# A hybrid decoder layer on one core: GpSimd's large operations to VectorE and ScalarE, Y evicted straight into its block tile, A's gates beside the SSD, x's first tile loaded first

## The chip, the cores and the metric

The kernel runs on one core of a Trainium2 chip. TensorE (PE) multiplies matrices, VectorE (DVE), ScalarE (ACT) and GpSimd (POOL) do the rest, and SyncE (SP) issues most of the DMAs. Each engine takes its instructions strictly in the order in which they stand on its queue, and waits on semaphores for the other engines. The metric is the device time of one execution in microseconds, the median of the runs taken.

## The reference, cut to what matters

One layer for a prompt of 1024 tokens and 8 samples of 8 tokens (1088 columns in all, T). One projection feeds four head groups, and a second one mixes them:

```python
z = jnp.einsum('bld,de->ble', x, p['w_in'])          # 1024 -> all columns of A, B, C, D
(a_x, a_gate, b_xbc, b_dt, b_gate, c_qkv, c_beta, c_decay, c_gate, d_u, d_gate) = split_cols(z, IN_SPLITS)
ya = rglru_mixer(a_x)  * silu(a_gate)                # A: conv of width 4, gated linear scan
yb = rms_norm(ssd_mixer(b_xbc, b_dt) * silu(b_gate)) # B: Mamba-2 SSD, chunked scan, 4 heads x 64
yc = gdn_mixer(c_qkv, c_beta, c_decay) * silu(c_gate)# C: gated DeltaNet, chunked
yd = s5_mixer(d_u) * silu(d_gate)                    # D: S5, 16 groups x 64 complex states
out = concat(ya, yb, yc, yd) @ w_out
x = layer_norm(ALPHA * x + out)
# inside gdn_mixer, for each chunk and head: a triangular inverse
tmat = triangular_solve(eye + m, eye, lower=True, unit_diagonal=True)
value, kcum = tmat @ (beta * v), tmat @ (beta * exp(decay) * k)
# inside s5_mixer: h_t = a * h_{t-1} + B u_t (complex, diagonal), y = Re(C h) + D u
```

The new states of the convs, the scans and S5 are returned as well.

## The kernel before

Each of x's eight k-tiles (128x1088) is split into a high part `xh` (ACT) and a low part `xl` (DVE); each weight strip likewise into `wh` and `wl`. A strip of 128 output columns is three blocks of tokens (320, 384, 384), each of 8 x 3 matmuls (xh.wh, xl.wh, xh.wl: L226 to L228 for most strips, L374 to L376 for S5's input, L398 to L400 for the token-major strip of small columns). Work comes in this order:

- **Start.** SP's queue loads the first halves of two S5 weight strips (`wr`), then x's first three k-tiles; POOL's queue loads `s5p`, `hv`, `pcol`. PE begins with S5's input strips (`pu`, L374).
- **S5's tables and the token strip.** DVE builds S5's constants, then `table(0)`, the powers of the state's factor (doubling, 42 small complex products, L463 to L465 in `cmul`). `outs(hf)` (L618 to L620) are six products of 128x512 on POOL. `half_run(hf)` multiplies by the table (`cm`, `gd`), scans (L650), multiplies back into `H`, and PE forms `y` from `H` and `outs` (L672, L676). `gemm_tok` runs beside half 0: nine token blocks of 24 matmuls (L398), each emptied by ACT (L403 to L406), gated by DVE (L407) and sent to DRAM (`bgd`) from a rotating buffer `bg`. `table(1)` and `outs(1)` are both on POOL and go on beside the gemms of C's strips.
- **C's strips** go through `gemm_strip`, `conv_of` and norms. `copy_out` empties PSUM: three copies of four on ACT (L242), the fourth on DVE (L244). `keep_tail` copies each strip's last columns on POOL (L270, L271).
- **The chunks of C** (from 208 us): for each of 8 prompt chunks of 128 tokens and one of 64, `prep` and `invert`, then `state`. `invert` runs six levels (three for the short chunk, 51 in all) of a block inversion for 4 heads. In one level PE forms T (L855), DVE masks it into `T` (L857) and copies its two diagonal blocks into `tb` (L846); PE accumulates X (L862), ACT evicts it (L864); PE accumulates Y (L867), ACT evicts it (L868); DVE copies Y's two diagonal blocks into `yb` (L846, `spread`), which the next level's L862 needs as its stationary side. `al`, the low part of A, comes from POOL (L839), as does `kd` (L801).
- **Beside the chunks** a second stream, `side`, gives PE its long matmuls: A's RG-LRU with the SSD's strips (`ahead`) merged in, then A's two gate strips, the SSD's four convs, and the SSD's chunks merged with the four gate strips of D and C (`gates_cd`). `merge` deals out yields by shares written beside each stream. `project` multiplies by w_out (L1426 to L1428) and does the LayerNorm: DVE adds and takes statistics, POOL raises to the power (L1437) and applies gain and bias (L1443, L1444), except for the last tile, where DVE does it (L1448, L1450).

A scheduling layer fixes each engine's order while the program is built; what an engine executes is that list, in order.

## Time and profile before

| | us |
|---|---|
| median of 3 runs | 653.14 |
| the runs | 653.14, 647.74, 653.92 |
| the profiled execution | 648.38 |
| its span, first to last instruction | 646.5 |
| PE busy | 589.7 (91%) |
| DVE busy | 469.6 (73%) |
| ACT busy | 271.6 (42%) |
| POOL busy | 180.9 (28%) |

The profile is one execution. Of each engine it tells the busy time, what ended each idle stretch (the releaser), and the clock granted to PE (1.00 is 2.4 GHz, half of that 1.2 GHz). Idle time counts only on an engine that the end of the program waits for, so PE's waits are read first, with their place in time. Busy time of PE is modelled from starts and sizes.

### The profile page before, as it was taken

Reading aid. Unit: us, or ns where it says so; the run is one execution under the profiler, and the core shown is the slowest. Engines: PE = TensorE matmul, PEld = TensorE weight load, DVE = VectorE, ACT = ScalarE, POOL = GpSimd, SP = SyncE. Lnnn points to the kernel's source line nnn. Section 1 sums busy time; section 2 is a strip of 40 time slices with the busy share of each in tenths; the row PEclk is TensorE's granted clock in tenths of the full one; section 3 lists DMA queues with packets and bytes.
Section 4 is the critical chain, followed back from the end, with each engine's and each line's share of the span. In section 5 each row is a group of like instructions: output and inputs, shape, how many; then the busy total and the mean of one; then the engine's idle time right before and its main releaser. Section 6 shows DMA issues by size and latency. Waiting matters only on the chain.

```text
span 646.5 us, 11718 instructions
## 1 busy us (share of the span) xinstructions
PE 589.7 (91%) x4284; PEld 504.0 (78%) x4284; DVE 469.6 (73%) x1378; ACT 271.6 (42%) x677; POOL 180.9 (28%) x305
## 2 busy tenths in 40 slices
...
GB/s 288 165 191 63 41 34 86 1 96 59 128 57 55 18 36 33 33 18 19 33 69 68 33 89 66 1 17 43 9 75 78 171 43 49 33 55 113 66 117 78
DMA packets 23929, 44.11 MB, mean 68 GB/s; under 512 B 3073, under 2 KB 10193, under 8 KB 23873
## 3 DMA queue, kind: packets, MB, share of 16 engines
q1 hardware_dynamic: 23696, 42.71, 20.1%
...
## 4 chain that ended last, share of the span: by engine, by line
PE 66%; DVE 19%; POOL 5%; issue 5%; ACT 2%; DMA 1%; SPq 0%; DVEq 0%; ACTq 0%; POOLq 0%
PE pg L226 8%; PE pg L227 8%; PE pg L228 8%; PE pg L1428 5%; PE pg L1427 5%; PE pg L1426 5%; DVE tb L846 2%; DVE yb L846 2%; DVE acc L266 2%; PE ssq L755 1%; PE pg L398 1%; DMA x<-in_x_t_dram 1%; PE pg L399 1%; PE pg L400 1%; PE kq L817 1%
## 5 line engine op out<-in xcount | busy, mean ns | idle before, releaser
L226 PE MATMUL pg<-xh,wh 128*128 128x384 f32 (+1 forms) x432 | 150.2, 348 | 9.0 <-DVE z L244 9.0
L227 PE MATMUL pg<-xl,wh 128*128 128x384 f32 (+1 forms) x432 | 149.0, 345 | 0.0
L228 PE MATMUL pg<-xh,wl 128*128 128x384 f32 (+1 forms) x432 | 147.0, 340 | 0.0
L226 PEld LDWEIGHTS pg<-xh,wh 128*128 128x128 f32 x432 | 82.8, 192 | 12.5 <-DVE z L244 9.3
L227 PEld LDWEIGHTS pg<-xl,wh 128*128 128x128 f32 x432 | 82.6, 191 | 2.1 <-issue 0.5
L228 PEld LDWEIGHTS pg<-xh,wl 128*128 128x128 f32 x432 | 82.4, 191 | 1.3 <-issue 0.3
L1426 PE MATMUL pg<-woh,wh 128*128 128x512 f32 (+1 forms) x144 | 58.2, 404 | 1.9 <-ACT wh L1415 1.9
L1427 PE MATMUL pg<-wol,wh 128*128 128x512 f32 (+1 forms) x144 | 58.5, 406 | 0.2
L1428 PE MATMUL pg<-woh,wl 128*128 128x512 f32 (+1 forms) x144 | 57.9, 402 | 0.4 <-DVE wl L1416 0.4
L266 DVE SCALAR_TENSOR_TENSOR acc<-z,pcol,acc 128x1112 f32<-128x1112 f32 x36 | 49.6, 1381 | 5.1 <-ACT acc L264 4.8
L864 ACT ACTIVATE XY<-XY 128x256 f16<-128x256 f32 (+1 forms) x51 | 19.4, 381 | 53.8 <-PE XY L862 48.2
L156 ACT ACTIVATE wh<-wr 128x512 fp32r<-128x512 f32 (+1 forms) x40 | 25.2, 633 | 35.0 <-PE pg L227 28.3
L1429 DVE SCALAR_TENSOR_TENSOR y<-y,pg 128x512 f32<-128x512 f32 (+1 forms) x18 | 12.3, 686 | 32.2 <-PE pg L1428 28.4
L1426 PEld LDWEIGHTS pg<-woh,wh 128*128 128x128 f32 (+1 forms) x144 | 26.6, 184 | 8.9 <-ACT wh L1415 2.2
L1428 PEld LDWEIGHTS pg<-woh,wl 128*128 128x128 f32 (+1 forms) x144 | 26.6, 185 | 7.3 <-DVE wl L1416 0.9
L1427 PEld LDWEIGHTS pg<-wol,wh 128*128 128x128 f32 (+1 forms) x144 | 26.5, 184 | 7.2 <-DVE wol L1393 1.0
L157 DVE TENSOR_TENSOR wl<-wr,wh 128x512 fp32r<-128x512 f32 (+1 forms) x40 | 28.2, 704 | 2.8 <-ACT wh L156 2.4
L857 DVE TENSOR_TENSOR T<-T,lev 128x256 f16<-128x256 f32 (+1 forms) x51 | 21.4, 419 | 10.7 <-PE T L855 10.1
L868 ACT ACTIVATE XY<-XY 128x256 f16<-128x256 f32 (+1 forms) x51 | 19.4, 381 | 22.5 <-PE XY L867 22.5
L242 ACT ACTIVATE z<-pg 128x384 f32<-128x384 f32 (+2 forms) x37 | 14.0, 389 | 34.5 <-PE pg L228 33.2
L846 DVE COPY tb<-T 64x256 f16<-64x256 f16 x99 | 26.2, 264 | 1.6
L846 DVE COPY yb<-XY 64x256 f16<-64x256 f16 x99 | 23.8, 240 | 4.4 <-ACT XY L868 3.0
...
## 6 DMA issues: line engine op xcount, KB each, us to landing
...
```

The costliest lines, as they stand in the source:

```text
L156: act(hv_, wv, AF.Copy)
L157: lo_eng[0].tensor_tensor(lv, wv, hv_.bitcast(F32), OP.subtract)
L226: mm(o, whi[k], xh[:, k, a:b], start=(k == 0), stop=False)
L227: mm(o, whi[k], xl[:, k, a:b], start=False, stop=False)
L228: mm(o, wlo[k], xh[:, k, a:b], start=False, stop=(k == 7))
L266: stt(acc[:, :CL], s[:, j:j + CL], col(wkey, j * nt + i), acc[:, :CL], OP.mult, OP.add)
L846: V.tensor_copy(dst[s, :, s], src[s])
L857: tt(t_[:n], pt[:n], lev[:n, l].unsqueeze(1).to_broadcast([n, 4, 64]), OP.mult)
L864: act(XY[:n, :256], px[:n, :256], AF.Copy)
L1426: mm(ps[:n], mh[k_], woh[:, k_, e], start=(k_ == 0), stop=False)
L1427: mm(ps[:n], mh[k_], wol[:, k_, e], start=False, stop=False)
L1428: mm(ps[:n], ml[k_], woh[:, k_, e], start=False, stop=(k_ == 7))
```

## The change

- **GpSimd's large operations go away from it.** `outs` (6 products each, both halves), `table(1)`, `al`, the decay of the sample states (L966, L1177) and LayerNorm's gain and bias go to DVE (the latter in halves of 512 columns); `kd` and the SSD's D term go to ACT as four scaled copies of 128x64 each; the square of A's factor (L1211) and the tails go to ACT.
- **Copies out of PSUM** are all on ACT; the every-fourth copy on DVE is gone.
- **Y** is evicted by ACT directly from PSUM into the two diagonal blocks of `yb`, then once more as the whole tile `Y`; DVE's two copies are gone, and the last level makes no `yb`.
- **A's gate strips** stand after the SSD's convs, in the stream that is merged with the SSD (share 66.0 where it was 44.0).
- **The start**: x's first k-tile is loaded first and split in three blocks; `s5p`, `hv` and `pcol` are loaded on SP's queue between x's tiles.

```diff
+    def x_load(k):
+        xs[k] = strip(cs, name="x")[:, :T]
+        nc.sync.dma_start(xs[k], I["x_t"][k])
     def x_split(k):
+        for a, b in BLOCKS if k == 0 else ((0, T),):
+            act(xh[:, k, a:b], x[:, a:b], AF.Copy)
+            tt(xl[:, k, a:b], x[:, a:b], xh[:, k, a:b].bitcast(F32), OP.subtract)
...
     def copy_out(dst, src):
-        flip[0] += 1
-        if flip[0] % 4:
-            act(dst, src, AF.Copy)
-        else:
-            V.tensor_copy(dst, src)
+        act(dst, src, AF.Copy)
...
-        G.dma_start(s5p, I["s5_par"])
-        G.dma_start(hv, I["heads"])
-        G.dma_start(pcol, I["columns"])
+        x_load(0)
         for i in range(2):
             w_part(i, 0)
-        for k in range(3):
-            x_split(k)
+        x_split(0)
+        x_load(1)
+        nc.sync.dma_start(s5p, I["s5_par"])
...
-                G.tensor_tensor(x, *u, OP.mult)
-                G.tensor_tensor(y, *v, OP.mult)
-                G.tensor_tensor(lo[:, j], x, y, OP.subtract)
+                tt(x, *u, OP.mult)
+                tt(y, *v, OP.mult)
+                tt(lo[:, j], x, y, OP.subtract)
...
-                     tuple(tab[:, j, :, s - 1:s].to_broadcast([P, 4, s]) for j in range(2)), [4, s], *((V, V) if hf == 0 else (G, G)))
+                     tuple(tab[:, j, :, s - 1:s].to_broadcast([P, 4, s]) for j in range(2)), [4, s])
...
-            G.tensor_tensor(h4(kd[:n]), h4(kh[:n]), bc(ed[:n, ti], 64), OP.mult)
+            for h in range(4):
+                act(h4(kd)[:n, h], h4(kh)[:n, h], AF.Copy, scale=ed[:n, ti, h:h + 1])
...
-                G.tensor_tensor(al[s, :, s], A[s, :, s], ah[s, :, s], OP.subtract)
+                tt(al[s, :, s], A[s, :, s], ah[s, :, s], OP.subtract)
...
-                act(XY[:n, 256:], px[:n, 256:], AF.Copy)
-                X, Y = pk(XY[:, :256]), pk(XY[:, 256:])
-                spread(yb, Y)
+                if l < (2 if n == NS else 5):
+                    for s in blocks:
+                        act(yb[s, :, s], pY[s], AF.Copy)
+                Y = pk(f16("Y", "Y", 256, 2))
+                act(Y[:n], pY[:n], AF.Copy)
...
-        yield from merge((ssd(bw, up, zb[0:2], zb[2], zb[3]), 40.0), (gates_cd(), 44.0))
+        yield from merge((ssd(bw, up, zb[0:2], zb[2], zb[3]), 40.0), (gates(), 66.0))
...
-                G.tensor_tensor(y[:n], y[:n], lnp[0][:n], OP.mult)
-                G.tensor_tensor(y[:n], y[:n], lnp[1][:n], OP.add)
+                for e in (slice(0, 512), slice(512, 1024)):
+                    tt(y[:n, e], y[:n, e], lnp[0][:n, e], OP.mult)
+                    tt(y[:n, e], y[:n, e], lnp[1][:n, e], OP.add)
```

**Place 1: DVE after table(0).** On DVE's queue before, the last product of the table (`tab`) is followed by the products with G (`G` holds PE's sums, `gd` the result), and the two token gates L407; `bg_112` is the buffer that goes back to ACT.

```order
236 L465 TENSOR_TENSOR tab_157_985<-cm_184_1053,cm_185_1054 128x4x64
237 L463 TENSOR_TENSOR cm_200_1108<-tab_157_985,G_194_1082 128x512
238 L464 TENSOR_TENSOR cm_201_1109<-tab_157_985,G_194_1082 128x512
239 L463 TENSOR_TENSOR cm_202_1113<-tab_157_985,G_194_1082 128x512
240 L465 TENSOR_TENSOR gd_199_1107<-cm_200_1108,cm_201_1109 128x512
241 L464 TENSOR_TENSOR cm_203_1114<-tab_157_985,G_194_1082 128x512
242 L407 SCALAR_TENSOR_TENSOR bg_112_650<-bg_112_650 128x256
```

The same place after (L468 to L470 are the lines of `cmul` now, L623 to L625 those of `outs`, L412 the gate's):

```order
233 L623 TENSOR_TENSOR cm_190_1076<-bk_27_169,s5p_4_94 128x512
234 L470 TENSOR_TENSOR tab_157_989<-cm_184_1057,cm_185_1058 128x4x64
235 L624 TENSOR_TENSOR cm_191_1077<-bk_27_169,s5p_4_94 128x512
236 L623 TENSOR_TENSOR cm_192_1081<-bk_27_169,ctn_87_358 128x512
237 L625 TENSOR_TENSOR lo_189_1075<-cm_190_1076,cm_191_1077 128x512
238 L624 TENSOR_TENSOR cm_193_1082<-bk_27_169,s5p_4_94 128x512
239 L625 TENSOR_TENSOR lo_189_1075<-cm_192_1081,cm_193_1082 128x512
240 L468 TENSOR_TENSOR cm_200_1112<-tab_157_989,G_194_1086 128x512
241 L469 TENSOR_TENSOR cm_201_1113<-tab_157_989,G_194_1086 128x512
242 L412 SCALAR_TENSOR_TENSOR bg_112_654<-bg_112_654 128x256
```

DVE now does the six products of `outs(0)` itself, and the gate stands behind two of the products with G where it stood behind five.

**Place 2: DVE at the end of S5's second half.** Before, the copy of one block of a C strip out of PSUM (`z_297` from `pg_304`) stands behind the products that give `H`:

```order
315 L463 TENSOR_TENSOR cm_278_1445<-tab_230_1300,gd_272_1422 128x512
316 L464 TENSOR_TENSOR cm_279_1446<-tab_230_1300,gd_272_1422 128x512
317 L463 TENSOR_TENSOR cm_280_1450<-tab_230_1300,gd_272_1422 128x512
318 L465 TENSOR_TENSOR H_277_1441<-cm_278_1445,cm_279_1446 128x4x128
319 L464 TENSOR_TENSOR cm_281_1451<-tab_230_1300,gd_272_1422 128x512
320 L658 COPY sf_89_358<-H_277_1441 128x4
321 L463 TENSOR_TENSOR cm_283_1458<-pw_47_232,H_277_1441 128x32
322 L465 TENSOR_TENSOR H_277_1441<-cm_280_1450,cm_281_1451 128x4x128
323 L244 COPY z_297_1564<-pg_304_1579 128x256
```

After, the same copy stands on ACT's queue, and nothing of S5 is ahead of it there:

```order
114 L264 ACTIVATE acc_356_1875<-z_287_1474,pcol_6_96 128x1112
115 L270 ACTIVATE tails_354_1863<-z_287_1474 128x3
116 L244 ACTIVATE z_297_1568<-pg_304_1583 128x8x8
117 L244 ACTIVATE z_297_1568<-pg_304_1583 128x256
118 L271 ACTIVATE tails_354_1863<-z_297_1568 128x24
```

while DVE has the end of `table(1)` and `outs(1)` ahead of the products with G, with one weight split (L157) among them:

```order
352 L623 TENSOR_TENSOR cm_263_1391<-bk_27_169,s5p_4_94 128x512
353 L470 TENSOR_TENSOR tab_230_1304<-cm_257_1372,cm_258_1373 128x4x64
354 L624 TENSOR_TENSOR cm_264_1392<-bk_27_169,s5p_4_94 128x512
355 L623 TENSOR_TENSOR cm_265_1396<-bk_27_169,ctn_87_358 128x512
356 L625 TENSOR_TENSOR lo_262_1390<-cm_263_1391,cm_264_1392 128x512
357 L624 TENSOR_TENSOR cm_266_1397<-bk_27_169,s5p_4_94 128x512
358 L157 TENSOR_TENSOR wl_368_1950<-wr_366_1947,wh_367_1949 128x512
359 L625 TENSOR_TENSOR lo_262_1390<-cm_265_1396,cm_266_1397 128x512
360 L468 TENSOR_TENSOR cm_273_1427<-tab_230_1304,G_267_1401 128x512
```

**Place 3: ACT in the inversion.** After, ACT's rows of one chunk's levels read so (L870 evicts X, L876 the two blocks of `yb`, L878 the whole Y); before there were two rows a level, L864 and L868.

```order
230 L876 ACTIVATE yb_2326<-XY_496_2874 64x4x64 x2
231 L878 ACTIVATE Y_500_2897<-XY_496_2874 128x256
232 L870 ACTIVATE X_503_2912<-XY_496_2874 128x256
233 L876 ACTIVATE yb_2326<-XY_496_2874 64x4x64 x2
234 L878 ACTIVATE Y_512_2962<-XY_496_2874 128x256
```

ACT's list grows by 200 instructions, POOL's shrinks by 140, and DVE's count is nearly the same (1375 for 1381).

## Rows read from the trace of the kernel before

**Rows 1.** The page: busy time of each engine; chain that ended last, by engine.

```profile
PE 589.7 (91%) x4284; PEld 504.0 (78%) x4284; DVE 469.6 (73%) x1378; ACT 271.6 (42%) x677; POOL 180.9 (28%) x305
...
PE 66%; DVE 19%; POOL 5%; issue 5%; ACT 2%; DMA 1%; SPq 0%; DVEq 0%; ACTq 0%; POOLq 0%
```

**Rows 2.** PE's waits over the span: total us, times, longest.

```profile
PE pg L374 <- ACT xh L187: 10.5, 1, 10.5
PE pg L226 <- DVE z L244: 9.0, 1, 9.0
PE XY L862 <- DVE yb L846: 6.6, 5, 5.0
PE pg L398 <- ACT bg L403: 5.8, 1, 5.8
PE XY L862 <- DVE T L857: 3.1, 4, 1.4
```

**Rows 3.** Windows: PE, PEld, DVE, ACT, POOL busy (x), clock, DMA share, GB/s.

```profile
0.00:10.00 10.00, 0.00 (x0) 0.00 (x0) 3.96 (x21) 3.17 (x4) 8.27 (x29) 1.00 0.77 273
20.00:60.00 40.00, 40.00 (x315) 39.70 (x314) 36.38 (x182) 21.11 (x46) 6.76 (x22) 1.00 0.49 144
208.00:576.00 368.00, 344.45 (x2779) 275.74 (x2778) 294.94 (x838) 171.44 (x468) 86.10 (x130) 0.99 0.15 48
570.00:640.00 70.00, 67.65 (x291) 54.18 (x290) 28.89 (x84) 16.21 (x44) 32.75 (x19) 1.00 0.22 83
```

**Rows 4.** Timeline of the start: start, us, engine, line, instruction [idle before <-releaser].

```profile
0.81 0.86 SPq L353 DMA_DIRECT2D wr<-in_w_tiles_dram  x2
...
3.99 1.31 ACT L355 ACTIVATE wh<-wr 128x512 fp32r<-128x512 f32 x2 [1.90 <-DMA wr<-in_w_tiles_dram]
...
9.37 1.11 ACT L187 ACTIVATE xh<-x 128x1088 fp32r<-128x1088 f32 x1 [4.08 <-DMA x<-in_x_t_dram]
...
10.54 0.64 PE L374 MATMUL pg<-xh,wh 128*128 128x320 f32 x1 [10.54 <-ACT xh L187]
```

**Rows 5.** Timelines of DVE, ACT and PE about the token strip.

```profile
51.79 0.23 DVE L628 COPY tab<-u 128x4 f32<-128x4 f32 x2
...
54.29 0.29 DVE L597 TENSOR_TENSOR kk<-kst,kk 128x128 f32<-128x128 f32 x1 [0.94 <-PE kst L596]
...
59.47 1.28 DVE L464 TENSOR_TENSOR cm<-tab 128x256 f32<-128x256 f32 x1
60.78 1.17 DVE L465 TENSOR_TENSOR tab<-cm,cm 128x256 f32<-128x256 f32 x1
64.39 1.53 DVE L463 TENSOR_TENSOR cm<-tab,G 128x512 f32<-128x512 f32 x1 [2.43 <-POOL lo L620]
...
67.55 0.68 DVE L463 TENSOR_TENSOR cm<-tab,G 128x512 f32<-128x512 f32 x1
68.16 0.68 DVE L465 TENSOR_TENSOR gd<-cm,cm 128x512 f32<-128x512 f32 x1
...
69.36 0.41 DVE L407 SCALAR_TENSOR_TENSOR bg<-bg 128x256 f32<-128x256 f32 x1
...
71.62 0.39 ACT L403 ACTIVATE bg<-pg 128x268 f32<-128x268 f32 x1 [11.82 <-DMA bgd<-bg]
...
65.86 0.28 PE L399 MATMUL pg<-wh,xl 128*128 128x268 f32 x1
65.98 0.28 PE L400 MATMUL pg<-wl,xh 128*128 128x268 f32 x1
72.07 0.59 PE L398 MATMUL pg<-wh,xh 128*128 128x268 f32 x1 [5.81 <-ACT bg L403]
...
75.58 0.43 PE L398 MATMUL pg<-wh,xh 128*128 128x268 f32 x1
```

**Rows 6.** Timelines of DVE and PE about the second half of S5.

```profile
102.59 1.34 DVE L279 SCALAR_TENSOR_TENSOR z<-z,acc 128x1024 f32<-128x1024 f32 x1 [0.72 <-ACT z L277]
...
117.15 1.53 DVE L463 TENSOR_TENSOR cm<-tab,G 128x512 f32<-128x512 f32 x1 [10.38 <-POOL lo L620]
...
128.65 0.68 DVE L465 TENSOR_TENSOR H<-cm,cm 128x512 f32<-128x512 f32 x1
...
129.72 0.69 PE L226 MATMUL pg<-xh,wh 128*128 128x384 f32 x1 [8.96 <-DVE z L244]
...
135.43 0.34 PE L226 MATMUL pg<-xh,wh 128*128 128x384 f32 x1
135.96 0.63 PE L672 MATMUL y<-U,tz 128*128 128x136 f32 x4
136.52 0.73 PE L676 MATMUL y<-H,lo 64*128 64x136 f32 x8
```

**Rows 7.** Timeline of one level of the inversion at its fastest: PE, ACT, DVE.

```profile
410.03 0.29 PE L862 MATMUL XY<-T,yb 128*128 128x64 f16 x4
...
411.16 0.38 ACT L868 ACTIVATE XY<-XY 128x256 f16<-128x256 f32 x1 [0.36 <-PE XY L867]
...
411.62 0.46 DVE L846 COPY yb<-XY 64x256 f16<-64x256 f16 x2
...
412.53 0.28 PE L862 MATMUL XY<-T,yb 128*128 128x64 f16 x4
...
413.33 0.28 PE L867 MATMUL XY<-XY,tb 128*128 128x64 f16 x4
```

**Rows 8.** Timelines of DVE and POOL about 536 us.

```profile
533.49 2.51 DVE L846 COPY tb<-T 64x256 f16<-64x256 f16 x2
536.02 2.63 DVE L846 COPY yb<-XY 64x256 f16<-64x256 f16 x2
...
533.57 2.33 POOL L1443 TENSOR_TENSOR y<-y,ln 64x1024 f32<-64x1024 f32 x1 [1.54 <-ACT y L1442]
```

**Rows 9.** Groups by line and form, whole span: busy, mean ns.

```profile
L157 DVE TENSOR_TENSOR wl<-wr,wh 128x512 fp32r<-128x512 f32 x36 | 25.3, 704 | 2.8 <-ACT wh L156 2.4
L846 DVE COPY yb<-XY 64x256 f16<-64x256 f16 x99 | 23.8, 240 | 4.4 <-ACT XY L868 3.0
L857 DVE TENSOR_TENSOR T<-T,lev 128x256 f16<-128x256 f32 x48 | 20.1, 419 | 9.2 <-PE T L855 8.6
```

**Rows 10.** ACT's groups by line and form, 200 to 580 us.

```profile
L944 ACT ACTIVATE qd<-ks,ea 128x64 f32<-128x64 f32 x28 | 6.5, 311 | 1.0 <-DVE R L941 1.0
...
L897 ACT ACTIVATE x<-J 64x256 f32<-64x256 f32 x8 | 3.0, 379 | 11.2 <-PE J L896 11.1
```

More of the change, by code (lines that the diff above doesn't have):

```diff
@@ L182, in hybrid_step @@
     xl = xp.tile([P, 8, T], F32R, name="xl", tag="xl")
+    xs = {}
+    def x_load(k):
+        xs[k] = strip(cs, name="x")[:, :T]
+        nc.sync.dma_start(xs[k], I["x_t"][k])
     def x_split(k):
-        x = strip(cs, name="x")[:, :T]
-        nc.sync.dma_start(x, I["x_t"][k])
-        act(xh[:, k], x, AF.Copy)
-        tt(xl[:, k], x, xh[:, k].bitcast(F32), OP.subtract)
+        x = xs.pop(k)
+        for a, b in BLOCKS if k == 0 else ((0, T),):
+            act(xh[:, k, a:b], x[:, a:b], AF.Copy)
+            tt(xl[:, k, a:b], x[:, a:b], xh[:, k, a:b].bitcast(F32), OP.subtract)
     def columns():
@@ L269, in keep_tail @@
     def keep_tail(s, dst):
-        G.tensor_copy(dst[:, 0:3], s[:, 1024:1027])
-        G.tensor_copy(dst[:, 3:27].rearrange("p (b e) -> p b e", e=3), seqs(s[:, 1027:SW])[:, :, 8:11])
+        act(dst[:, 0:3], s[:, 1024:1027], AF.Copy)
+        act(dst[:, 3:27].rearrange("p (b e) -> p b e", e=3), seqs(s[:, 1027:SW])[:, :, 8:11], AF.Copy)
     def silu_compact(s, acc):
@@ L356, in w_part @@
             tt(l_, wr, h_.bitcast(F32), OP.subtract)
-        G.dma_start(s5p, I["s5_par"])
-        G.dma_start(hv, I["heads"])
-        G.dma_start(pcol, I["columns"])
+        x_load(0)
         for i in range(2):
             w_part(i, 0)
-        for k in range(3):
-            x_split(k)
+        x_split(0)
+        x_load(1)
+        nc.sync.dma_start(s5p, I["s5_par"])
+        x_split(1)
+        x_load(2)
+        nc.sync.dma_start(hv, I["heads"])
+        nc.sync.dma_start(pcol, I["columns"])
+        x_split(2)
         for i in range(2):
@@ L367, in u_tiles @@
         for k in range(3, 8):
+            x_load(k)
             x_split(k)
@@ L627, in table @@
             for j in range(2):
-                (V if hf == 0 else G).tensor_copy(tab[:, j, :, 0], u8[:, j, q0:q0 + 4])
+                V.tensor_copy(tab[:, j, :, 0], u8[:, j, q0:q0 + 4])
             s = 1
@@ L862, in invert @@
                     mm(pX[:n, h], idh[:n, :n] if Y is None else yb[:n, h, :n], t_[:n, h], start=False, stop=False, skip_group_check=True)
-                XY = f16("XY", "XY", 512, 2)
-                act(XY[:n, :256], px[:n, :256], AF.Copy)
+                X = pk(f16("X", "X", 256, 2))
+                act(X[:n], pX[:n], AF.Copy)
                 yield 0.2
@@ L1094, in chunk @@
             y = r1("y")
-            G.tensor_tensor(h4(y)[:n], h4(xt)[:n], bc(hv[:n, 16:20], 64), OP.mult)
+            for h in range(4):
+                act(h4(y)[:n, h], h4(xt)[:n, h], AF.Copy, scale=hv[:n, 16 + h:17 + h])
             tt(y[:n], py[:n, :256], y[:n], OP.add)
@@ L1210, in rglru @@
             q = strip(up, name="aq")
-            G.tensor_tensor(q[:, :CL], a_[:, :CL], a_[:, :CL], OP.mult)
+            act(q[:, :CL], a_[:, :CL], AF.Square)
             stt(r[:, :CL], q[:, :CL], 1.0, r[:, :CL], OP.add, OP.mult)
@@ L1352, in side @@
         yield from merge((rglru(bw, up, xc, hA), 20.0), (ahead(), 44.0))
-        for i in range(2):
-            g = yield from gate(C_AG + P * i, up)
-            stt(toks(g[:, :NS]), toks(g[:, :NS]), 0.5, seqs(hA[i][:, NP:CL])[:, :, 3:11], OP.mult, OP.mult)
-            stt(g[:, NS:T], g[:, NS:T], 0.5, hA[i][:, :NP], OP.mult, OP.mult)
-            mix[i] = g
         tails = new_tails()
```

12 lines of the change are left out of this document (9 added, 3 removed).

## The prediction

> **What bounds the kernel now.** I read the page first: PE is busy 91% of the span and holds 66% of the chain that ended last, DVE 19% of it, POOL 5% with 28% busy [rows 1]. So PE is the engine to relieve, and what can be won without less PE work is its idle time, some 57 us, and the slow clock behind long idle stretches. PE's waits name the places [rows 2]: 10.5 us at the start for the first split tile of x, 5.8 us for a token buffer, 9.0 us for one copy on DVE, and 9.7 us at L862, the matmul that consumes `yb` and `T`. The windows then say where a gain would stay: PE has no idle time at all from 20 to 60 us, 23.6 us of it in the chunks of C (208 to 576, 344.45 busy of 368), and 2.4 in 570 to 640 [rows 3]. DVE is busy 295 of those 368 us, ACT only 171, so DVE is the one that is late there.
>
> The sum is made against the profiled execution, 648.4 us.
>
> **Start and token strip.** Before, two weight parts are loaded ahead of three x tiles; the first tile lands at 9.37 with all three in flight, ACT needs 1.11 for it, PE starts at 10.54 [rows 4]. After, x's first tile (544 KB) goes first and alone. By the row of the two weight parts (512 KB issued from 0.81, used at 3.99) it lands near 4.1, and at the 273 GB/s of that window [rows 3] the 512 KB behind it take 1.9 us more; a weight split is 0.65 (1.31 for two). First matmul about 5.7, so 4.8 us earlier. The three small loads that move to SP's queue stand ahead of x's second tile, which so lands hardly earlier than before; PE has 18 matmuls on the first tile, enough to cover that. PE is unbroken from 20 to 60, so it reaches its token wait (from 72.07 - 5.81 = 66.3) at 61.5.
>
> There it waits for a buffer `bg` whose gate L407 is late on DVE: DVE ends table(0) at 61.95 (60.78 + 1.17), waits 2.43 for POOL's `outs(0)`, starts the gate at 69.36; the buffer's DMA lets ACT go at 71.62, PE at 72.07 [rows 5]. Two products of the table take 1.28 and 1.17 while POOL works, where a like size takes 0.42 (L857) [rows 9]: 1.6 us. DVE after: it starts on x about 1.5 us earlier (a choice, between 0 and the 4.8 of PE, since it is nearly full from 20 to 60), two weight splits of 0.7 [rows 9] stand behind the gate on its new list, and the 1.6 goes: table(0) ends at 61.95 - 1.5 - 1.4 - 1.6 = 57.4. Then six products of `outs(0)` at the 0.61 between starts of such products (67.55, 68.16) = 3.7, two products with G 1.2, the gate 0.41: 62.7. The buffer's way from the gate's end to ACT was 1.85 (71.62 - 69.77), to PE 0.45: PE resumes at 65.0 against 72.07, **-7.1**. Behind the 5.81 us of idle PE ran slower: 16 matmuls from 72.07 to 75.58, 0.22 between starts against 0.12 before the wait (65.86, 65.98): 1.6 lost. A 3.5 us wait is left, so I give back half: **-0.8**. Together **-7.9**; ends -5 (DVE gains nothing from the start) and -11 (PE's whole 4.8 reaches DVE and the clock stays).
>
> **S5's second half.** Before, PE stood 8.96 us to 129.72 for the copy L244 that is queued on DVE behind all products of `H`; DVE itself had stood 10.38 for POOL's `outs(1)`. The 24 matmuls that follow took 6.24 us (129.72 to 135.96), at the 0.175 of the last three (135.43 to 135.96) they take 4.2: 2.0 for the clock [rows 6]. On ACT the copy waits for nothing of S5. The whole 11.0 would go, if PE's next consumer of DVE, the `y` matmuls L676 at 136.52, finds `H` ready. DVE's way there: the strip whose conv stands ahead is done at 103.9 (102.59 + 1.34), now 96.0; table(1) on DVE takes what table(0) took, 51.79 to 61.95 less the 1.6 above and 0.94 of waiting = 7.6, so 103.6; `outs(1)` 3.7 and the split among them 0.6: 107.9; the products to `H` 12.2 before (117.15 to 129.33), of which 2 were the two long first rows beside POOL: 118.1. PE: idle began at 120.76, now 112.9, plus 4.2 and 0.56 for L672: 117.6. It waits 0.5. So **-10.5**; ends -2 (DVE comes 8 us later, the copy's stall returns as a wait for `H`) and -11.
>
> From 141 to 208 PE is full before; the gain passes through.
>
> **The chunks of C.** Of 23.6 us idle, 9.7 are L862's. One place shows the worst: at 533 to 538 a `tb` pair takes 2.51 and a `yb` pair 2.63 beside POOL's two LayerNorm products, where 0.46 is usual, and PE stands 5.0 [rows 2, 7, 8]. After, DVE does these products itself, four of 0.68, 2.7 us of queue: 2.3 gained, and about 1 for the clock behind it. In each level DVE loses the `yb` pair (23.8 us in all) and gains `al` (17 x 0.42, by the like-sized L857) and small products; ACT gains two evictions of 64x256, 0.38 each [rows 9, 10]. From Y's matmul to `yb` it was ACT 0.38 and DVE 0.46 with a hop between (411.16 to 412.08 = 0.92); now two ACT evictions, 0.7. The saving in latency is only 0.2 a level, and the level at its fastest takes 2.5 us, most of it PE's own work; the rest of the gain is a DVE with some 25 us less to do. I take 5 of the 18 us that remain idle, so **-8**; ends 0 and -16 (two thirds of the idle).
>
> ACT pays: 82 block evictions at 0.34 between starts 28, 72 scaled copies (`kd` and D's term, 9 chunks x 4 heads each) at 0.31 [rows 10] 22, strips' copies, tails and the square about 15 (estimates from the same sizes): 65 us in 360 on an engine that was 47% busy there, so some 65% after.
>
> A rule speaks against this. The Trainium skill, "ScalarE: Activation LUTs", Rules for kernel authors, says adds and multiplies belong on VectorE rather than ScalarE. The page's price (186 ns and 0.833 per element) would be 399 ns for a block eviction, and the row above (379) agrees; by the page's figure the sum stays as it is.
>
> **The end.** From 570 PE is full; LayerNorm on DVE adds 6 x 2.7 = 16 us to 28.9 of 70 [rows 3] and hides under PE. The last tile was on DVE already: 0. A's gates beside the SSD move no work from PE; they change what covers a wait, and are counted in the chunks' ends.
>
> **Sum.** 648.4 - 7.9 - 10.5 - 8 = 622.0. The median of the runs is 0.7% above the profiled execution, its lowest run below it; I add 1.5, between 0 and 4.6: **623.5 us**.
>
> **Rivals.**
> - *The chunks gain nothing* (18%): ACT's evictions queue as DVE's did, DVE at 75% still comes late with `T` and `tb`. For it: `T` alone has 3.1 of PE's waits. 623.5 + 8 = 631.5.
> - *S5's stall returns as a wait for `H`* (8%): table(1) and outs(1) are now serial on DVE, every us that DVE comes later than PE is a us. Against it: DVE stood idle for 10.38 us there [rows 6], and table(1) with outs(1) is 11.9. 623.5 + 8.5 = 632.
> - *The chunks gain twice as much* (15%): L862's waits and DVE's other delays go together, 615.
> - *Slower: ACT becomes the inversion's bound* (7%). Y's whole tile is now evicted behind two block evictions, 0.7 later, and X's of the next level behind that. If a level lengthens by 0.6, 51 levels cost 31 and the gain of 8 is not there: 662. It decides from 0.37 a level (18.4 of gains elsewhere over 51 levels), with the 1% 0.5. Against it: Y was evicted at 411.54 and its consumer ran at 413.33 [rows 7], 1.8 us of slack, and ACT's four evictions make 1.4 in a level of 2.5. The rule above is the same mechanism.
>
> **Numbers.** My forecast, 617 to 629, has 52%. Range 609 to 640: it holds the forecast, the first two rivals and most of the third, 85%, and takes in the ends of the terms, of which not all come together. About 1% is what a measurement can tell: under 646.6 is faster, 88%; within 1% 6%, slower 6%, both from the last rival's degrees.
>
> **What would show it.** PE's first matmul near 5.7. PE's wait at the token strip under 4 us instead of 5.8, and ended near 65. No wait for a copy near 112; a wait of L681 (the `y` matmul) for `H` of 0 to 2. In the chunks, `yb` from ACT, no `tb` pair above 0.6 beside LayerNorm, and PE's idle time 12 to 18 us. I am wrong if PE waits for ACT's Y evictions by more than 10 us in the chunks, or for `H` by more than 4, or if DVE's tail after 640 grows.

## The result, and the profile after

The changed kernel takes **621.07 us** (median; 620.11 to 628.62) against 653.26 (647.74 to 653.92) for the kernel before beside it: a ratio of 0.9569, 95% interval 0.9515 to 0.9623. Forecast were 623.5 us and a range of 609 to 640. Its profiled execution took 620.72 with a span of 619.0, against 648.4 and 646.5. The one run at 628.62 had a mean granted clock of 0.974, the other three, at 620.11 to 621.41, one of 0.986 to 0.988.

The page after, with the busy time of each engine and the chain that ended last by engine, answers to [rows 1]:

```profile
PE 586.3 (95%) x4284; PEld 503.4 (81%) x4284; DVE 464.9 (75%) x1372; ACT 325.0 (53%) x877; POOL 62.7 (10%) x165
...
PE 65%; DVE 16%; ACT 8%; issue 6%; DMA 3%; POOL 2%; SPq 1%; DVEq 0%; ACTq 0%; POOLq 0%
```

DVE is hardly less busy (464.9, before 469.6), since it took over work from POOL; ACT has 53 us more, POOL 118 less. PE does the same 4284 matmuls in 27.5 us less span, and has 32.7 us of the span idle where it had 56.8. PE's waits (total us, times, longest), to be set against [rows 2]:

```profile
PE pg L379 <- ACT wh L355: 6.1, 1, 6.1
PE XY L868 <- ACT Y L878: 3.3, 13, 0.4
PE pg L1439 <- ACT wh L1428: 3.1, 1, 3.1
PE pg L403 <- ACT bg L408: 2.7, 1, 2.7
PE yT L1144 <- DVE y L1140: 2.0, 5, 0.6
PE XY L868 <- DVE T L863: 1.6, 2, 1.2
```

The 9.0 for the copy L244 and the single 5.0 for `yb` are gone. ACT's eviction of Y is waited for 13 times, never over 0.4.

For the places of the prediction, I divide the span by four rows of PE: the last matmul of the token strip, the last `y` matmul of S5, the first `T` matmul of the inversions, and the last matmul of the output projection. Times of after are from its timeline, those of before from the same rows there:

| stretch of PE | before, us | after, us | change | forecast |
|---|---|---|---|---|
| start to the end of the token strip | 82.93 | 74.46 | -8.5 | -7.9 |
| to the end of `y` | 58.3 | 48.1 | -10.2 | -10.5 |
| to the first `T` matmul | 71.7 | 75.6 | **+3.9** | 0 |
| to the last projection matmul | 425.9 | 413.4 | **-12.5** | -8 |
| to the end of the span | 7.7 | 7.4 | -0.3 | 0 |
| sum | 646.5 | 619.0 | -27.5 | -26.4 |

So the total, 27.5, came within 1.1 us of the forecast 26.4, but by luck: out of two errors of 4 with opposite signs. The experiments are about these two.

The last long stretch, as windows of the two traces (length; PE, PEld, DVE, ACT, POOL busy (x), clock, DMA share, GB/s). Before:

```profile
207.00:639.00 432.00, 408.23 (x3052) 326.67 (x3051) 320.18 (x910) 185.15 (x505) 117.93 (x146) 0.99 0.16 54
```

and after:

```profile
192.00:612.00 420.00, 405.24 (x3056) 327.75 (x3054) 311.46 (x857) 234.63 (x682) 37.15 (x78) 1.00 0.17 56
```

PE's idle time fell from 23.8 to 14.8, 9.0 us; the same matmuls were busy 3.0 us less, which goes with a clock of 1.00 for 0.99 behind fewer waits. DVE has only 8.7 us less to do there, ACT 49.5 more.

One more view of before and after stands behind most of what follows. I took every DVE instruction that overlaps a GpSimd instruction in time and summed by how much it exceeds the median of its own line and shape, where it does: 22.8 us before, 2.6 after. (DVE instructions that overlap none exceed it by only 1.5 us in all before, 2.1 after.) I call this sum **drawn-out DVE time**; it is worked out from all rows of a trace, and is no row itself.

### The profile page after: what moved, and what is told of

It reads as the page before. It is cut to its first block, busy times and chain, and to the rows that moved or that the text cites. A ratio compares the mean times of both kernels' runs of the same rounds, so it can differ in the third digit from the quotient of the medians.

```text
span 619.0 us, 11787 instructions
## 1 busy us (share of the span) xinstructions
PE 586.3 (95%) x4284; PEld 503.4 (81%) x4284; DVE 464.9 (75%) x1372; ACT 325.0 (53%) x877; POOL 62.7 (10%) x165
## 4 chain that ended last, share of the span: by engine, by line
PE 65%; DVE 16%; ACT 8%; issue 6%; DMA 3%; POOL 2%; SPq 1%; DVEq 0%; ACTq 0%; POOLq 0%
PE pg L234 7%; PE pg L232 7%; PE pg L233 7%; PE pg L1441 5%; PE pg L1440 5%; PE pg L1439 5%; DVE acc L266 2%; ACT yb L876 2%; PE ssq L760 1%; DMA wr<-in_w_tiles_dram 1%; PE XY L868 1%; DVE cm L469 1%; PE pg L403 1%; DVE cm L468 1%; PE pg L405 1%
## 5 line engine op out<-in xcount | busy, mean ns | idle before, releaser
L233 PE MATMUL pg<-xl,wh 128*128 128x384 f32 (+1 forms) x432 | 147.1, 341 | 0.0
L156 ACT ACTIVATE wh<-wr 128x512 fp32r<-128x512 f32 (+1 forms) x40 | 25.2, 632 | 32.8 <-PE pg L233 26.4
L876 ACT ACTIVATE yb<-XY 64x256 f16<-64x256 f32 x82 | 31.0, 378 | 15.6 <-PE XY L873 13.3
L1439 PEld LDWEIGHTS pg<-woh,wh 128*128 128x128 f32 (+1 forms) x144 | 26.4, 183 | 10.2 <-ACT wh L1428 3.5
L870 ACT ACTIVATE X<-XY 128x256 f16<-128x256 f32 (+1 forms) x51 | 19.5, 383 | 27.5 <-PE XY L868 27.2
L244 ACT ACTIVATE z<-pg 128x384 f32<-128x384 f32 (+2 forms) x48 | 17.5, 396 | 25.1 <-PE pg L234 23.6
L157 DVE TENSOR_TENSOR wl<-wr,wh 128x512 fp32r<-128x512 f32 (+1 forms) x40 | 27.8, 697 | 2.2 <-ACT wh L156 1.8
L742 ACT ACTIVATE gam<-gam,nac 128x128 f32<-128x128 f32 (+1 forms) x72 | 21.0, 374 | 5.9 <-PE gam L739 5.9
L403 PE MATMUL pg<-wh,xh 128*128 128x268 f32 x72 | 20.7, 288 | 2.7 <-ACT bg L408 2.7
```

The costliest lines, as they stand in the source:

```text
L156: act(hv_, wv, AF.Copy)
L157: lo_eng[0].tensor_tensor(lv, wv, hv_.bitcast(F32), OP.subtract)
L233: mm(o, whi[k], xl[:, k, a:b], start=False, stop=False)
L403: mm(o, xh[:, k, c0:c0 + P], whi[k], start=(k == 0), stop=False)
L876: act(yb[s, :, s], pY[s], AF.Copy)
L1439: mm(ps[:n], mh[k_], woh[:, k_, e], start=(k_ == 0), stop=False)
```

## Experiments

Theory 1 is the prediction's: the gain in the chunks is the relief of DVE's queue, the `yb` pairs first. Theory 2: it is GpSimd's work beside DVE, which draws DVE's instructions out wherever both run, so that every large GpSimd operation given away pays, and Y's place matters little. Theory 3: A's gate tiles beside the SSD give PE matmuls to run in the waits. "T to projection" below is the stretch of 425.9 us before and 413.4 after, each from one trace. Its own scatter is small: three kernels below in which PE's list from the first T matmul on is the changed kernel's (`after_no_start`, `after_no_s5`, `warm`) have 413.4 to 415.1 with it. Medians scatter more (the changed kernel's own runs over 8 us), and for Y, the gates and the start the intervals of the ratios overlap the changed kernel's, so those parts rest on the traces.

**One part of the change undone at a time.**

Y's eviction as before (three rows of it):

```diff
-                    for s in blocks:
-                        act(yb[s, :, s], pY[s], AF.Copy)
+                spread(yb, Y)
```

> The changed kernel with Y's eviction as before: ACT evicts Y whole, DVE copies its two blocks into yb. The chunks of C gained 12.5 us. Theory 1, the queue: the gain came from taking the yb pair off DVE's queue, then this kernel is 8 to 10 us slower than the changed one (about 630) and PE's waits for yb from DVE come back. Theory 2, the shared port: the gain came from GpSimd's large operations being gone, then it stays within 2 us of 621. Theory 3, the cover: the gain came from A's gates beside the SSD, then it stays within 2 us of 621.

624.60 us (624.32 to 628.6; ratio to before 0.9621, 0.9567 to 0.9675), 3.5 over the changed kernel; T to projection 417.3, that is 3.9 longer, less than theory 1 said and more than the others did. Theory 1 as a main cause falls: nearly 9 of the 12.5 us stay with `yb` on DVE.

GpSimd gets its work in the chunks back (tails, `kd`, `al`, state decays, D's term, the square, LayerNorm):

```diff
-                tt(al[s, :, s], A[s, :, s], ah[s, :, s], OP.subtract)
+                G.tensor_tensor(al[s, :, s], A[s, :, s], ah[s, :, s], OP.subtract)
...
-                    tt(y[:n, e], y[:n, e], lnp[0][:n, e], OP.mult)
+                G.tensor_tensor(y[:n], y[:n], lnp[0][:n], OP.mult)
```

> The changed kernel with the operations of the chunks, the SSD, the tails and LayerNorm back on GpSimd (kd, al, D term, state decay, the square, the tails, gain and bias). Theory 2, the shared port: DVE copies beside GpSimd's LayerNorm take 2 us again and the kernel is 9 to 12 us slower than the changed one (about 632). Theory 1, the queue: it is 2 to 4 us slower (about 624). Theory 3: about 623.

The four runs took 630.97, 635.79, 641.53 and 641.92 us; the trace is that of 635.79, 15 over the changed kernel's. In it T to projection is 429.4, 16.0 longer than after and even 3.5 longer than before. Drawn-out DVE time is back at 18.4 us (the next expectation has 18.8). PE's waits there are for DVE again:

```profile
PE yT L1142 <- DVE y L1138: 5.2, 5, 1.7
PE XY L867 <- DVE T L862: 4.6, 6, 1.7
PE XY L867 <- ACT Y L877: 3.6, 15, 0.4
```

Theory 2 holds, and at more than it expected: DVE does less in that kernel than in the changed one (296.7 us busy in the stretch against 306.7), and is waited for more. In this pair not how much work stands in DVE's queue, but how long GpSimd holds up single pieces of it, is what the path feels.

LayerNorm's two products alone back on GpSimd:

```diff
-                for e in (slice(0, 512), slice(512, 1024)):
-                    tt(y[:n, e], y[:n, e], lnp[0][:n, e], OP.mult)
-                    tt(y[:n, e], y[:n, e], lnp[1][:n, e], OP.add)
+                G.tensor_tensor(y[:n], y[:n], lnp[0][:n], OP.mult)
+                G.tensor_tensor(y[:n], y[:n], lnp[1][:n], OP.add)
```

> The changed kernel with LayerNorm's gain and bias back on GpSimd, all else as changed. The kernel with all of the chunks' operations back on GpSimd was some 15 us slower by its span (634.1 against 619.0), and DVE's instructions were drawn out by 18.8 us in all, 6.5 of it from 520 to 560 where LayerNorm runs. Theory 2a, LayerNorm's long products carry it: 5 to 7 us slower than the changed kernel (about 627). Theory 2b, the many short ones (al, kd, D) in the inversion's chain carry it: 1 to 2 us slower (about 622.5).

631.91 us (630.04 to 632.43; 0.972, 0.9668 to 0.9772), more than theory 2a expected; the span is 9.3 longer, all of it from LayerNorm's first tile on. Up to 515 us PE's rows are the changed kernel's in the same order, and at 508 us they stand within 0.3 us of theirs, so another order of PE's list is no rival here. The timeline where a tile's LayerNorm meets the inversion, as it did in [rows 8] (the held DVE rows from a narrower window, which does not merge them with their neighbours):

```profile
511.98 0.28 DVE L1429 TENSOR_TENSOR wl<-z,wh 128x128 fp32r<-128x128 f32 x1
...
513.42 2.38 POOL L1456 TENSOR_TENSOR y<-y,ln 64x1024 f32<-64x1024 f32 x1 [1.54 <-ACT y L1455]
513.49 2.46 DVE L1429 TENSOR_TENSOR wl<-gate,wh 128x128 fp32r<-128x128 f32 x1
...
515.87 2.47 POOL L1457 TENSOR_TENSOR y<-y,ln 64x1024 f32<-64x1024 f32 x1
516.07 2.42 DVE L1429 TENSOR_TENSOR wl<-z,wh 128x128 fp32r<-128x128 f32 x1
519.02 0.41 DVE L863 TENSOR_TENSOR T<-T,lev 128x256 f16<-128x256 f32 x1
519.58 0.37 PE L868 MATMUL XY<-T,yb 128*128 128x64 f16 x4 [4.49 <-DVE T L863]
```

A weight split that takes 0.28 elsewhere takes 2.46 beside one GpSimd product, and another 2.42 beside the next. The product for `T` stands behind them in DVE's queue, and PE stands 4.49 us. What follows runs at a lower clock: 0.75 in the 10 us behind the wait, where the changed kernel averages 1.00 over the stretch:

```profile
510.00:520.00 10.00, 5.36 (x42) 3.66 (x41) 9.57 (x26) 4.06 (x10) 5.38 (x3) 0.91 0.05 12
520.00:530.00 10.00, 9.57 (x62) 6.69 (x62) 5.57 (x18) 5.55 (x17) 0.00 (x0) 0.75 0.23 67
```

The Trainium skill, "SBUF — State Buffer", Who interferes with whom, says that only the port pair shared by VectorE and GpSimd causes contention, and that it is an exclusive lock. The rows agree as far as they go: each held DVE instruction starts just behind GpSimd's product (by 0.07 and 0.20) and ends 0.15 after it. That nothing else contends, no run here shows.

A's gate tiles ahead of the SSD, as before:

```diff
+        for i in range(2):
+            g = yield from gate(C_AG + P * i, up)
...
-        yield from merge((ssd(bw, up, zb[0:2], zb[2], zb[3]), 40.0), (gates(), 66.0))
+        yield from merge((ssd(bw, up, zb[0:2], zb[2], zb[3]), 40.0), (gates_cd(), 44.0))
```

> The changed kernel with A's two gate strips ahead of the SSD's convs again. Theory 3, the cover: PE's waits at the SSD's and the chunks' short matmuls grow, 6 to 10 us slower (about 629). Theories 1 and 2: within 2 us of 621, since no work moves between engines.

630.34 us (626.08 to 637.19; 0.9673, 0.9588 to 0.9759). In the trace, of the run at 626.08, the span is 5.4 longer, T to projection 5.3. Theory 3 holds for a part of it. Drawn-out DVE time stays at 2.5, so this is another mechanism than theory 2. Which one is not shown whole: PE's idle time in the stretch grew by only 1.7 us (14.4 to 16.1) and the clock lost the same, so the rest lies in PE's modelled busy time.

S5's second table and `outs` back on GpSimd:

```diff
-                tt(x, *u, OP.mult)
-                tt(y, *v, OP.mult)
-                tt(lo[:, j], x, y, OP.subtract)
+                G.tensor_tensor(x, *u, OP.mult)
+                G.tensor_tensor(y, *v, OP.mult)
+                G.tensor_tensor(lo[:, j], x, y, OP.subtract)
```

> The changed kernel with outs of both halves and table(1) back on GpSimd. If the second half's gain hangs on H as I worked it out, the token gate comes 4 to 5 us later and PE, which no longer waits for the copy, waits for H instead: 10 to 12 us slower (about 632), with a PE wait at the y matmul of 5 us or more. Rival: moving the copies to ACT was enough, H is not waited for, only the token gate is late: 4 us slower (about 625).

630.22 us (629.39 to 632.9; 0.97, 0.9649 to 0.9752), 9 over the changed kernel; `y` ends at 133.9 for 122.6. The 5.8 wait of the token strip is back, and a second one came elsewhere than I had said, at a copy:

```profile
106.99 1.22 DVE L279 SCALAR_TENSOR_TENSOR z<-z,acc 128x1024 f32<-128x1024 f32 x1 [0.72 <-ACT z L277]
108.25 1.11 ACT L757 ACTIVATE sq<-z 128x1088 f32<-128x1088 f32 x1 [1.29 <-DVE z L279]
...
110.37 0.50 ACT L244 ACTIVATE z<-pg 128x64 f32<-128x64 f32 x2
...
110.92 0.44 PE L232 MATMUL pg<-xh,wh 128*128 128x384 f32 x1 [4.35 <-ACT z L244]
```

The copy is on ACT now, but ACT runs in order too: the square ahead of it waits for DVE's conv, which is late since DVE was drawn out between 80 and 100 us, by 6.1 in the sum above. A copy moved to ACT is freed from DVE's queue only if ACT's own queue holds nothing that waits for DVE.

The start as before (x behind the weights, tile unsplit):

```diff
-        x_load(0)
         for i in range(2):
             w_part(i, 0)
-        x_split(0)
...
+        for k in range(3):
+            x_split(k)
```

> The changed kernel with the loads of the start as before. If the start reaches the end of the program by way of DVE's table and the token gate: 2 to 4 us slower than the changed one (about 624), table(0) on DVE ends 2 to 3 us later. Rival: the start is hidden by the waits behind it, within 1 us of 621.

625.31 us (623.07 to 628.16; 0.9618, 0.9566 to 0.967), 4.2 over the changed kernel: PE's first matmul at 8.89 for 6.10 and `y` done at 124.9 for 122.6. Of the 2.8 us of the start 2.4 are still there at `y`; the 4.2 of the medians is more than the start itself.

**Parts of the change alone, on the kernel before.**

Copies to ACT and all of S5 to DVE (the edits of `copy_out`, `outs` and `table`):

```diff
-        flip[0] += 1
-        if flip[0] % 4:
-            act(dst, src, AF.Copy)
-        else:
-            V.tensor_copy(dst, src)
+        act(dst, src, AF.Copy)
```

> The kernel before with two parts of the change: all copies out of PSUM on ACT, and outs and table(1) on DVE. By my working of the two S5 stalls the token strip ends 4 to 6 us earlier and the second half's y another 9 to 10: 13 to 16 us faster than before (about 637 to 639). Rival: the chunks give part of it back, since the work there is reordered: 8 to 10 us faster (about 643).

641.57 us (641.0 to 642.46; 0.9867, 0.9822 to 0.9912), 7.5 less than the kernel before beside it: half of the main expectation, and close to the rival's 8 to 10. The first `T` matmul came 11.6 us earlier (201.4 for 212.9), but T to projection became 430.3, 4.4 longer. The chunks took that back; the same 5.0 wait beside LayerNorm stood at 531.88.

LayerNorm alone to DVE:

```diff
-                G.tensor_tensor(y[:n], y[:n], lnp[0][:n], OP.mult)
-                G.tensor_tensor(y[:n], y[:n], lnp[1][:n], OP.add)
+                for e in (slice(0, 512), slice(512, 1024)):
+                    tt(y[:n, e], y[:n, e], lnp[0][:n, e], OP.mult)
+                    tt(y[:n, e], y[:n, e], lnp[1][:n, e], OP.add)
```

> The kernel before with LayerNorm's gain and bias alone moved from GpSimd to VectorE. Putting them back on GpSimd cost the changed kernel 9.3 us of span, all of it after the start of the projection. If their cost is the same in the kernel before: 6 to 9 us faster than before (about 643), PE's wait of 5.0 us beside LayerNorm is gone. Rival: DVE, which here still has the yb pairs, now holds the chain up by these products itself: 0 to 3 us faster (about 648).

639.81 us (639.5 to 640.88; 0.9854, 0.981 to 0.99): T to projection 418.1, 7.8 shorter, and the 5.0 wait gone (the longest for `yb` is 0.8). Here too PE's list is the same, up to 542 us. PE's idle time in the stretch fell by 5.5 (23.3 to 17.8), and the 3.4 us that the clock had lost behind the wait are back. Five lines of code carry more than half of the chunks' gain, with DVE given *more* to do.

Y's eviction alone (X, `yb` and Y evicted by ACT as in the changed kernel):

```diff
-                spread(yb, Y)
+                if l < (2 if n == NS else 5):
+                    for s in blocks:
+                        act(yb[s, :, s], pY[s], AF.Copy)
```

> The kernel before with Y's eviction alone changed. My prediction's step, that the yb pair on DVE's queue is what PE waits for: 5 to 8 us faster than before (about 645). Rival, the shared port: the copies were late because GpSimd held them up, tb still is: 0 to 3 us faster (about 650), and a PE wait of some 3 to 5 us beside LayerNorm stays.

657.79 us (653.08 to 659.49), ratio 1.0111 (1.008 to 1.0142): **slower** than before by 1.1%, which neither expectation had; T to projection 429.9. The trace is of a run of 653.46, among the shorter ones. A wait of 1.46 at 475.86 is followed by a stretch at the lower of the clock's two levels (columns as above; the clock is the number after POOL's):

```profile
475.86 0.44 PE L1137 MATMUL yT<-idf,y 128*128 128x128 f32 x2 [1.46 <-DVE y L1133]
```

```profile
480.00:490.00 10.00, 10.00 (x39) 7.74 (x39) 3.64 (x13) 1.23 (x5) 2.15 (x3) 0.50 0.23 78
```

PE is busy for 10.00 of 10 there, at 0.50, that is 1.2 of the two levels of 1.2 and 2.4 GHz: half of the stretch is lost without a wait.

Y's eviction and LayerNorm together:

```diff
-                spread(yb, Y)
+                        act(yb[s, :, s], pY[s], AF.Copy)
...
-                G.tensor_tensor(y[:n], y[:n], lnp[0][:n], OP.mult)
+                    tt(y[:n, e], y[:n, e], lnp[0][:n, e], OP.mult)
```

> The kernel before with LayerNorm on VectorE and Y's eviction changed. Alone, Y's eviction made the kernel before 5 us slower; taken from the changed kernel it cost 3.5. If its worth hangs on GpSimd being off DVE: 2 to 4 us faster than LayerNorm alone. If ACT's evictions cost by themselves and the changed kernel only hides it: 3 to 6 us slower than LayerNorm alone. Third reading: the 5 us were PE's clock, at half level from 476 to 490 behind a 1.5 us wait, and say little on Y: within 1.5 us of LayerNorm alone.

651.36 us (646.66 to 655.59; 1.0008, 0.9971 to 1.0045): 11.5 over LayerNorm alone, more than any of the three readings had. Y's edit costs in a kernel with GpSimd's other work, with LayerNorm gone or not. Two stretches, at 430 to 450 and 480 to 500, ran at a lower clock behind waits of 1.08 (432.92) and 1.47 (480.12) for DVE, of which these are two windows:

```profile
440.00:450.00 10.00, 10.00 (x58) 7.85 (x57) 5.12 (x16) 3.54 (x11) 1.89 (x3) 0.62 0.13 41
...
480.00:490.00 10.00, 9.88 (x34) 8.10 (x34) 4.47 (x17) 0.62 (x2) 1.53 (x3) 0.58 0.18 56
```

A third place shows how small a DVE instruction GpSimd can hold:

```profile
258.63 2.03 POOL L1213 TENSOR_TENSOR aq<-acc 128x1112 f32<-128x1112 f32 x1
258.68 2.00 DVE L1002 TENSOR_TENSOR ors<-ors,rq 64x4 f32<-64x4 f32 x1 [1.16 <-POOL ors L1001]
261.06 0.85 DVE L879 TENSOR_TENSOR tb<-E,idp 64x256 f16<-64x256 f32 x2
261.96 0.29 PE L884 MATMUL F<-Y,tb 128*128 128x64 f16 x4 [2.24 <-DVE tb L879]
```

A product of 64x4 elements (0.16 elsewhere) took 2.00, and PE, two DVE instructions later, stood 2.24.

Y's eviction, LayerNorm and A's gates beside the SSD, the last as

```diff
-        yield from merge((ssd(bw, up, zb[0:2], zb[2], zb[3]), 40.0), (gates_cd(), 44.0))
+        yield from merge((ssd(bw, up, zb[0:2], zb[2], zb[3]), 40.0), (gates(), 66.0))
```

> The kernel before with LayerNorm on VectorE, Y's eviction changed, and A's gates beside the SSD. Without the gates this pair ran at 651 us, 11.5 slower than LayerNorm alone, with PE's clock at half level in the SSD's stretch (430 to 450, 480 to 500). If A's long gate matmuls beside the SSD are what keeps PE's waits there short and the clock up: the two stretches at half level are gone and it is 633 to 638 us. If Y's eviction costs by itself in a kernel whose GpSimd still does al, kd and D: it stays at 648 or above, with waits of PE at the SSD's transposes over 1 us.

649.63 us (648.5 to 651.01; 1.0008, 0.9979 to 1.0037): as the second reading had it, and by the ratio no faster than without the gates. The trace tells more. The same two windows:

```profile
440.00:450.00 10.00, 9.57 (x67) 7.58 (x66) 6.10 (x21) 4.23 (x13) 3.55 (x6) 1.00 0.04 12
...
480.00:490.00 10.00, 9.36 (x63) 7.59 (x63) 6.81 (x24) 1.64 (x5) 3.10 (x6) 1.00 0.30 111
```

With the gates' matmuls as cover the clock is 1.00 in both, and T to projection 423.7 instead of 430.9: 7.2 back. Against that, the first `T` matmul came 3.1 later than with Y and LayerNorm alone, ahead of what the two kernels differ in. The rest of the change is still missing: waits of 2.24 at 265 and 1.71 at 480.64 stay, each at the end of a chain through small GpSimd operations, and the stage is 10.3 longer than in the changed kernel.

**The start's rate.** The changed kernel with ten matmuls on zeros ahead of the first real one:

```diff
+        for _ in range(10):
+            mm(pw_, zw[:, :P], zw, start=True, stop=True)
```

> The changed kernel with ten matmuls of 512 columns on zeros (their result is not used) ahead of the first real one, while PE waits for its first tile. In the changed kernel PE starts 4.4 us earlier than before but reaches the token strip only 2.5 earlier, since its first matmuls stand 0.32 apart where 0.175 is usual. If that is the clock after idleness: the first tiles go at 0.175, PE reaches the token strip about 2 us earlier, DVE's table, which waits there for PE, with it, and the kernel is 1.5 to 2.5 us faster than the changed one (about 619). Rival: the loads of x and the splits set the pace there, or the token gate absorbs it: within 0.7 us of the changed kernel.

622.69 us (619.79 to 626.9; 0.9593, 0.9554 to 0.9632): no gain over 621.07. The first real matmuls do run at full rate (0.175 between starts, where the changed kernel has 0.32 until 13 us; the granted clock reads 1.00 from 6 to 15 us in both, so it does not show this), and then PE waits for data:

```profile
9.80 0.34 PE L385 MATMUL pu<-xl,wh 128*128 128x384 f32 x1
9.98 0.34 PE L386 MATMUL pu<-xh,wl 128*128 128x384 f32 x1
11.12 0.41 PE L384 MATMUL pg<-xh,wh 128*128 128x320 f32 x1 [0.80 <-ACT xh L193]
...
13.33 0.41 PE L385 MATMUL pg<-xl,wh 128*128 128x320 f32 x1 [0.95 <-DVE xl L194]
```

The loads and splits of x set the pace there, not the rate of the matmuls; the token strip's first matmul came 0.48 us earlier (33.47 for 33.95), and `y` at the same 122.6. No kernel of these was faster than the changed one.

## Why the prediction was right, and where its steps were not

**Start: right within 0.4, and it shrank on the way.** PE begins at 6.10, forecast 5.7:

```profile
4.81 0.47 ACT L193 ACTIVATE xh<-x 128x320 fp32r<-128x320 f32 x1 [2.73 <-DMA x<-in_x_t_dram]
5.42 0.63 ACT L355 ACTIVATE wh<-wr 128x512 fp32r<-128x512 f32 x1
6.10 0.64 PE L379 MATMUL pg<-xh,wh 128*128 128x320 f32 x1 [6.10 <-ACT wh L355]
```

That is 4.4 earlier than [rows 4], but the token strip began only 2.5 earlier (33.95 for 36.41). The cover itself held: the 18 matmuls on the first tile start from 6.10 to 12.56, with one wait of 0.51 for ACT's split of that tile, and the second tile's follow without a wait. What was lost is their rate: most stand 0.27 to 0.32 apart until 13 us, some 7 us, where before they did so for 4 (10.54 to 14.38). `warm` shows that the full rate would not have helped: PE is through with the first tile at 10.3 and waits 0.80 for the second. So "4.8 us earlier" was not carried on to the token wait, which began at 62.69 and not at 61.5. For the strip's end this did not matter, since PE waited there for DVE anyway.

**Token strip: right.** Forecast: gate at 62.7, PE on at 65.0. Measured:

```profile
62.62 0.41 DVE L412 SCALAR_TENSOR_TENSOR bg<-bg 128x256 f32<-128x256 f32 x1
...
64.90 0.39 ACT L408 ACTIVATE bg<-pg 128x268 f32<-128x268 f32 x1 [6.50 <-DMA bgd<-bg]
65.34 0.40 PE L403 MATMUL pg<-wh,xh 128*128 128x268 f32 x1 [2.65 <-ACT bg L408]
```

The wait is 2.65 for 5.81 in [rows 5]. The 0.8 of clock that I gave back was too little, the 1.6 came back whole: the clock was 1.00 from 60 to 80. PE went on 6.73 earlier (72.07 to 65.34, forecast 7.1), and the strip ended 8.47 earlier. Of the start, DVE gained 0.8 rather than the 1.5 that I chose: in `after_no_start` its table(0) starts at 50.18, here at 49.34.

**S5: right.** Forecast: `H` at 118.1, PE at 117.6. Measured:

```profile
116.09 0.68 DVE L470 TENSOR_TENSOR H<-cm,cm 128x512 f32<-128x512 f32 x1
117.31 0.63 PE L677 MATMUL y<-U,tz 128*128 128x136 f32 x4
117.86 0.39 PE L681 MATMUL y<-H,lo 64*128 64x136 f32 x2
```

The last product of `H` ends at 116.77, 1.1 before PE asks: the stall of [rows 6] did not return, -10.2 for -10.5. `after_no_s5` shows that the copies' move alone does not do it; S5's move without the copies' was not tried.

**"From 141 to 208 PE is full before; the gain passes through": the step that failed.** The stretch became 3.9 longer. PE came 18.5 us earlier to `glu` (138.2 for 156.7), and what it needs there, `gh` from ACT, came only 15.4 earlier (its second part starts at 137.90, before at 153.27):

```profile
137.90 2.10 ACT L711 ACTIVATE gh<-yt 128x1088 fp32r<-128x1088 f32 x2
139.04 0.93 PE L723 MATMUL glu<-gh,gh 128*128 128x320 f32 x4 [0.86 <-ACT gh L711]
140.37 0.41 PE L724 MATMUL glu<-gl,gh 128*128 128x320 f32 x1 [0.40 <-DVE gl L712]
...
141.57 0.42 PE L724 MATMUL glu<-gl,gh 128*128 128x320 f32 x1 [0.32 <-DVE gl L712]
```

These waits are 1.6 us. Then 36 matmuls of two columns, the sums of squares, take 5.07, and the matmuls behind them 0.32 from start to start instead of 0.175 (first row: the same 36 in the kernel before):

```profile
166.69 4.07 PE L755 MATMUL ssq<-half,sq 128*128 128x2 f32 x36
...
150.43 5.07 PE L760 MATMUL ssq<-half,sq 128*128 128x2 f32 x36
155.83 0.52 PE L233 MATMUL pg<-xl,wh 128*128 128x384 f32 x1
156.15 0.52 PE L234 MATMUL pg<-xh,wl 128*128 128x384 f32 x1
```

The clock of that window is 0.66 with PE busy for all of it:

```profile
150.00:160.00 10.00, 10.00 (x55) 10.00 (x54) 4.37 (x18) 2.50 (x8) 2.72 (x12) 0.66 0.29 110
```

In the kernel before the window behind the same matmuls reads

```profile
170.00:180.00 10.00, 10.00 (x53) 9.77 (x53) 7.98 (x26) 4.05 (x6) 2.95 (x12) 0.83 0.44 146
```

so the clock cost 3.4 there after and 1.7 before (10 us times what is missing to 1.00). 1.6 of waits and 1.7 of clock make 3.3 of the 3.9. "PE is full" said that it had no wait, not that its inputs had slack; a stretch through which a gain is to pass needs its inputs' own times read. The stretch is 74.7 to 77.3 in all kernels with the copies on ACT, and without that edit 71.7 or 71.8 in four (before, LayerNorm, Y, both) but 73.3 in the fifth (`y_ln_gates`); the copies alone were not tried, so their part is not shown.

**Chunks: mis-sized, and for the wrong reason.** The term was 2.3 for LayerNorm, 1 for its clock, 5 for the relief of DVE's queue, "the `yb` pair (23.8 us in all)" named first. Measured: LayerNorm 7.8 alone on the kernel before and 9.3 undone in the changed one; Y's eviction 3.9 in the changed kernel and -4.0, a loss, alone; A's gates, which I counted at nothing, 5.3. The step that failed for LayerNorm is "2.7 us of queue: 2.3 gained", with "about 1 for the clock behind it". It set DVE's own 2.7 against the 5.0, as if both lay on the path; `ln_only` got 5.5 of idle time and 3.4 of clock, of which 7.8 stayed. DVE's four products are separate instructions of 0.69, between which the inversion's go (at 515.10 the changed kernel has `T`'s product between them, at 516.03 the `tb` pair), while each of GpSimd's two held one DVE instruction to its own end. In the changed kernel no `tb` pair exceeds 0.5 us, as forecast. That PE's idle time would be 12 to 18 us held as well (14.8). Whether the 5 for DVE's queue was there is not shown: with Y's eviction undone the stretch is 3.9 longer, but PE's idle time in it only 0.9.

**The rivals.** That the chunks gain nothing did not come true. That they gain twice as much, 16, was nearer to the 12.5 (by 3.5) than the forecast 8 was (4.5); the 3.9 given back ahead of the chunks kept the total at the forecast. ACT did not become the inversion's bound: it was busy for 56% of the last long stretch (65% forecast), and PE waited 3.3 for its evictions of Y. For Y's eviction alone this rival had the sign right and the mechanism wrong: what is seen in that kernel is a wait for DVE and the slow clock behind it.

**The parts do not add.** Undoing single parts costs 3.9 (Y), 9.3 (LayerNorm), 5.3 (gates) and 16.0 (all of GpSimd's chunk work, LayerNorm in it) in a stretch that gained 12.5; adding them to the kernel before gives +4.0 (Y), -7.8 (LayerNorm), +5.0 (both), -2.2 (both and the gates).

**What stays open.** An edit can make the scheduling layer write the instructions of PE in another order; with Y's, 1674 of PE's 4284 rows differ from the kernel before, from the first chunk on. The traces show in what Y's loss consists: what the granted clock lacks to 1.00, summed over T to projection in windows of 2 us, is 3.4 us before, 8.5 with Y, 0.0 with LayerNorm and 15.4 with both, while PE's idle time is 23.3, 22.3, 17.8 and 17.9. Y's eviction added no idle time; its loss is the clock behind waits. How much of the 4 to 13 us is due to the order, and how much to ACT's evictions changing who runs beside GpSimd, no run here separates; nor why the clock stayed at its lower level for so long behind a wait of 1.5 us in `y_only` and not behind one of 1.71 in `y_ln_gates`, beyond that the gates' matmuls were there.
